# A list of experts ordered by token quarters in 15 classes; pieces that serve one quarter as plain fp32 products of 64 columns, two side by side

## The chip, the cores and the metric

The kernel runs on one core of a Trainium2 chip. The metric is the time of one execution on the device in microseconds. An execution is profiled apart from the timed ones, and its trace gives for every engine when each instruction ran.

## What is computed

Two transformer blocks over 256 tokens of width 2048, all in float32. The last part of the second block is the one that the change touches: a layer of 16384 single-neuron experts, of which each token uses 128 (8 heads with 16 each).

```python
def peer_ffn(hn, w_query, sub_keys, expert_down, expert_up):
    ...
    top_s, top_i = lax.top_k(scores, PEER_TOPK)
    cand_s = (top_s[:, :, 0, :, None] + top_s[:, :, 1, None, :]).reshape(...)
    cand_i = (top_i[:, :, 0, :, None] * PEER_N_KEYS + top_i[:, :, 1, None, :]).reshape(...)
    best_s, best_pos = lax.top_k(cand_s, PEER_TOPK)
    expert_idx = jnp.take_along_axis(cand_i, best_pos, axis=-1)
    gates = jax.nn.softmax(best_s, axis=-1)
    ...
        u = expert_down[idx]
        act = jax.nn.gelu(jnp.einsum('thkd,td->thk', u, xb), approximate=False)
        vv = expert_up[idx]
        return jnp.einsum('thk,thkd->td', (gb * act).astype(vv.dtype), vv)
```

## The kernel before

The kernel computes the expert layer densely where it can. A matrix G holds the gate of each token for each expert (zero where the token doesn't use it); all down projections are computed (jobs on `w_pd`, tile A4), and U is the product of activation and gate, turned so that a row is one expert with 256 tokens. The output is U times the up weights `w_pu`, a sum over experts in pieces of 128 rows of 2048 floats (1 MB).

Experts that no token uses are left out. `table_gen` notes which experts each half of the tokens uses (tiles `used0`, `used1`). `rank_gen` gives every expert a place in a list: first those that only the first half (tokens 0 to 127) uses, then those of both, then those of the second alone, then the unused. `u_gen` scatters each row of U to its place in a buffer in DRAM by an indirect DMA of GpSimd (L1716, 124 of them), each row with the expert's number behind its 256 values. The last four pieces of experts (`dense`) are not scattered.

The list is then worked off in 105 pieces (`UP_C`). Pieces 0 to 27 serve the first half alone, 28 to 76 both, 77 to 104 the second alone, whatever the data; if the classes don't fit these bounds, a flag `bad` is set and a branch behind the list, `all_experts`, computes everything anew. For each piece:

- SyncE loads 128 rows of the list (`urow`, L1799, 130 KB); seven buffers, up to two pieces ahead of the next step.
- GpSimd gathers the up weights of these experts with the numbers in `urow` (L1809, 1 MB, tile `ring`, six buffers).
- ScalarE and VectorE split both into a high and a low part in fp32r (`A5hi`, `A5lo`, L1830 and L1831; `wh`, `wl`, L1835 and L1836), three steps ahead of TensorE; a step is half a piece, 1024 of its columns.
- TensorE makes three fp32r products (low by high, high by high, high by low) of 128 by 512 for each of the four column blocks and each half of the tokens that the piece serves: 12 products for a piece and a half (`up_run`, L1863 to L1865). They add up in eight PSUM banks, four (`mm`) for the first half of the tokens and four (`aux`) for the second.

When the last product of a bank is done, `finish` adds the residual and stores the result. TensorE begins the stage with the four dense pieces (tile `ulast`), beside which the first pieces of the list are loaded. The instruction `memset` on L1820 is the fence behind which rows may be read from the list.

An engine runs its instructions in the order in which the code issues them. Side work (`rank_gen`, `u_gen`) is written as generators; `pump` advances each by one `yield` after every step of TensorE's main work.

Of the kernel before, what the change touches and what calls it, by code (L numbers as in the profile page):

```python
# [19 lines left out]
P = 128  # L20
# [19 lines left out]

UP_A, UP_B, UP_C = 77, 28, 105
TRASH = UP_C * P
# [139 lines left out]
class _Up:  # L182


    kc, before = 4, None

    def __init__(self, c, tiles, dense=False):
        self.c, self.tiles, self.dense = c, tiles, dense


@with_exitstack
def tile_kernel(ctx: ExitStack, tc: tile.TileContext, T, out):
# [83 lines left out]
    def run_jobs(jobs):  # L276
        units = []
        for j in jobs:
            for u in range(j.kc // 2):
                units.append((j, u))  # L280
        order = [j for j in jobs if isinstance(j, _Job) or j.dense]
        held = []
# [23 lines left out]
        def split(s):  # L306
            j, u = units[s]
            if isinstance(j, _Up) and not j.dense:
                sp[s] = up_split(j, u)
# [20 lines left out]
        for s, (j, u) in enumerate(units):  # L330
# [6 lines left out]
            if u == 0 and j.before is not None:  # L337
                j.before()
            wh, wl = sp.pop(s)
            if isinstance(j, _Up):  # L340
                if room == len(units):
# [1021 lines left out]
    def open_peer():  # L1363
# [11 lines left out]
        for n in ("i1T", "i2T", "gaT"):  # L1375
            pk[n] = pre.tile([P, S], F32, name=n)
        pk["F"] = [mp.tile([P, P], F32, name=f"used{t}") for t in range(2)]
        pk["st1"] = ExitStack()
# [132 lines left out]
    def table_gen():  # L1511

        with ExitStack() as es:
# [38 lines left out]
            def used(n):  # L1552
                per = S // TB // 2
                if n % per == 0:
                    dve.tensor_copy(acc, st["s", n])
                else:
                    dve.tensor_tensor(acc, acc, st["s", n], op=ALU.max)

            N = S // TB
            for n in range(N + 4):  # L1560
# [15 lines left out]
                if n < N:  # L1576
                    first(n)
                if n - 3 in (N // 2 - 1, N - 1):
                    for w in (4, 2):
                        dve.tensor_tensor(acc[:, :w], acc[:, :w], acc[:, w:2 * w], op=ALU.max)  # L1580
                    t = 0 if n - 3 < N // 2 else 1
                    F = pk["F"][t]
# [6 lines left out]
    def rank_gen():  # L1589


        spare = [pk["post"].tile([P, 8, P], F32, tag="gt", name=nm("spare"), bufs=6) for _ in range(2)]
        sl = lambda k: slice(k * P, (k + 1) * P)
        lt, b, far, over, s = (spare[0][:, k] for k in range(5))
        end = spare[0][:, 5, :1]
        e = spare[0][:, 6, :3]
        rs, ct = (spare[1][:, 3 * k:3 * k + 3].rearrange("p k c -> p (k c)") for k in range(2))
        d = rs
        F0, F1 = pk["F"]
        dve.tensor_tensor(b, F0, F1, op=ALU.mult)  # L1600
        dve.tensor_tensor(F0, F0, b, op=ALU.subtract)
        dve.tensor_tensor(F1, F1, b, op=ALU.subtract)
        cls = (F0, b, F1)
        rp, tp = aux(), aux()
        for k in range(3):
            pe.matmul(rp[:, sl(k)], cls[k], ones, start=True, stop=True)
        for k in range(3):
            pe.transpose(tp[:, sl(k)], cls[k], ident)
        yield
        act.copy(rs, rp[:, :3 * P])  # L1610
        act.copy(ct, tp[:, :3 * P])
        dve.tensor_tensor(lt, triu, ident, op=ALU.subtract)

        dve.tensor_copy(far, pk["ids"])
        dve.tensor_scalar(far, far, float(TRASH), None, op0=ALU.add)
        gp, np_ = aux(), aux()
        for k in range(3):
            pe.matmul(gp[:, sl(k)], cls[k], lt, start=True, stop=False)
            for q in range(k):
                pe.matmul(gp[:, sl(k)], ones, rs[:, sl(q)], start=False, stop=False)  # L1620
            pe.matmul(gp[:, sl(k)], lt, rs[:, sl(k)], start=False, stop=True)

        for k in range(3):
            for q in range(k + 1):
                pe.matmul(np_[:, sl(k)], ones, rs[:, sl(q)], start=q == 0, stop=q == k)
        yield

        dve.tensor_scalar(d, gp[:, :3 * P], float(-TRASH), None, op0=ALU.add)
        dve.tensor_tensor(d, d, ct, op=ALU.mult)
        dve.tensor_tensor(s, d[:, sl(0)], d[:, sl(1)], op=ALU.add)  # L1630
        dve.tensor_tensor(s, s, d[:, sl(2)], op=ALU.add)
        yield
        dve.tensor_scalar(over, s, 0.0, None, op0=ALU.is_ge)
        dve.tensor_scalar(s, s, 0.0, float(TRASH), op0=ALU.min, op1=ALU.add)
        dve.tensor_tensor(far, far, s, op=ALU.subtract)
# [4 lines left out]
        yield  # L1640
        dve.tensor_scalar(e[:, 0:1], np_[:, 0:1], float(UP_B * P), None, op0=ALU.is_lt)
        dve.tensor_scalar(e[:, 1:2], np_[:, P:P + 1], float(UP_A * P), None, op0=ALU.is_gt)
        dve.tensor_scalar(e[:, 2:3], np_[:, 2 * P:2 * P + 1], float(UP_C * P), None, op0=ALU.is_gt)
        dve.tensor_reduce(end, e, axis=AX.X, op=ALU.max)
        dve.tensor_copy(pk["bad"], end)

# [144 lines left out]

    up = {"loaded": 0, "rows": 0}
# [11 lines left out]
    def up_load(upto):  # L1804
        while up["loaded"] <= min(upto, len(ups) - 1):
            j = ups[up["loaded"]]
            rows_load(up["loaded"] + 2)
            j.raw = ring()
# [4 lines left out]
    def up_split(j, u):  # L1813
        if "fence" not in pk:
# [9 lines left out]
        e = ups.index(j)  # L1824
        if u == 0:
            up_load(e + 3)
            a, b = j.tiles[0] * P, (j.tiles[-1] + 1) * P

            j.hi, j.lo = (x[:, 0] for x in xt_tiles("A5", e % 4))
            act.copy(j.hi[:, a:b], j.u[:, a:b])  # L1830
            dve.tensor_tensor(j.lo[:, a:b], j.u[:, a:b], j.hi[:, a:b].bitcast(F32), op=ALU.subtract)  # L1831
        src = j.raw[:, u * 1024:(u + 1) * 1024]
        wh = wpool.tile([P, 1024], F32R, tag="wh", name=nm("wh"), bufs=4)
# [3 lines left out]
        return wh, wl  # L1837

    def up_run(j, u, wh, wl, tiles):
        if j.dense:  # L1840
            k = 0
            while "ulast" not in pk:
                pump()
                k += 1
                assert k < 1000
            hi, lo = (x[:, j.c - JL] for x in pk["ulast"])
        else:
            hi, lo = j.hi, j.lo
        if j is ups[-3] and u == 0:
            pk["over"] = nc.values_load(pk["bad"][0:1, 0:1], min_val=0, max_val=1)  # L1850
        for t in tiles:
            mine = [x for x in dense + ups if t in x.tiles]
            first, last = j is mine[0], j is mine[-1]
            if first and u == 0:
# [59 lines left out]


    alone = [_Up(c, (0,)) for c in range(UP_B)], [_Up(c, (1,)) for c in range(UP_A, UP_C)]
    both = [_Up(c, (0, 1)) for c in range(UP_B, UP_A)]
    dense = [_Up(JL + k, (0, 1), True) for k in range(4)]
    mid = alone[0][4:] + alone[1][:-4]
    ups = alone[0][:4]  # L1920
    while both or mid:
        ups += both[:1] + mid[:1]
        both, mid = both[1:], mid[1:]
    ups += alone[1][-4:]
    jobs += dense + ups
    run_jobs(jobs)
# [30 lines left out]
```

## Time and profile before

| | us |
|---|---|
| median of 3 runs | 3033.9 |
| lowest and highest | 3032.38, 3033.99 |
| the profiled execution's own time | 3032.62 |
| its span, first to last instruction | 3030.7 |
| TensorE busy in the span | 3006.2 (99%) |
| VectorE, ScalarE, GpSimd busy | 2013.5, 1652.9, 432.0 |

The span is read against the profiled execution's own time, which is 1.9 us longer. Times in the trace count from the span's start. A busy engine is one with an instruction in work; matmuls overlap, so the step from one start to the next, not the length of one, is what TensorE pays.

### The profile page before, as it was taken

The page shows a single profiled execution, that of the slowest core. Times are in us where ns is not written, and L with a number is a line of the kernel's source. Part 1 is how long each engine was busy: PE and PEld are TensorE (multiplying, and loading weights), DVE is VectorE, ACT ScalarE, POOL GpSimd, SP SyncE. Part 2 cuts the span into 40 slices and gives each one's busy share as a digit, 9 for nine tenths or more (in the row PEclk, how much of TensorE's full clock was granted, in tenths as well). Part 3 has the DMA queues.
Part 4 walks back from the last instruction along what each step waited for, and adds up shares of the span by engine and source line. Part 5 has one row for each costly group of instructions (what it writes and reads, how often), then busy time and mean ns, then how long its engine had stood idle before and what let it go on. Part 6 is the DMA issues. An engine that isn't in the chain of part 4 may idle for free. (4 is left out here: it accounts for less than half of the span.)

```text
span 3030.7 us, 39602 instructions
## 1 busy us (share of the span) xinstructions
PE 3006.2 (99%) x14715; PEld 2576.3 (85%) x14715; DVE 2013.5 (66%) x2890; ACT 1652.9 (55%) x2426; POOL 432.0 (14%) x496
## 2 busy tenths in 40 slices
PE   9999999999999999999999999999999999999998
PEld 7899988888888888898998888888888888888887
DVE  6876655566555557567656689877875555666666
ACT  7455545544444445565555544447774554555555
POOL 2310000000000000103111000000002664333332
PEclk9999999999999999999999999999999999999999
DMA  7344555555555555554455687666777997888886
GB/s 293 118 141 163 183 177 183 191 194 181 194 182 194 189 186 169 193 182 148 142 177 180 233 275 256 220 209 210 221 212 247 341 343 270 317 292 292 287 292 213
DMA packets 161868, 658.27 MB, mean 217 GB/s; under 512 B 15488, under 2 KB 63232, under 8 KB 103040
## 3 DMA queue, kind: packets, MB, share of 16 engines
q1 hardware_dynamic: 95808, 491.37, 47.9%
q0 software_dynamic: 21072, 126.62, 11.3%
q10 hardware_dynamic: 44784, 37.64, 3.7%
q8 instruction: 118, 1.93, 0.2%
q14 instruction: 86, 0.70, 0.1%
HBM read 600.97 MB, written 54.60 MB: 216 GB/s over the span
## 5 line engine op out<-in xcount | busy, mean ns | idle before, releaser
L325 DVE TENSOR_TENSOR wl<-raw,wh 128x1024 fp32r<-128x1024 f32 (+2 forms) x902 | 1061.8, 1180 | 822.8 <-ACT wh L324 778.3
L324 ACT CAST wh<-raw 128x1024 fp32r<-128x1024 f32 (+2 forms) x902 | 901.6, 1003 | 937.1 <-PE mm L374 866.9
L373 PE MATMUL mm<-wh,A4lo 128*128 128x512 f32 x1152 | 459.7, 399 | 0.0
L375 PE MATMUL mm<-wl,A4hi 128*128 128x512 f32 x1152 | 449.6, 390 | 0.0
L374 PE MATMUL mm<-wh,A4hi 128*128 128x512 f32 x1152 | 448.8, 390 | 0.0
L1836 DVE TENSOR_TENSOR wl<-ring,wh 128x1024 fp32r<-128x1024 f32 x210 | 256.9, 1226 | 142.1 <-ACT wh L1835 134.8
L1835 ACT CAST wh<-ring 128x1024 fp32r<-128x1024 f32 x210 | 219.9, 1050 | 179.4 <-PE aux L1864 154.7
L373 PE MATMUL mm<-wh,A2lo 128*128 128x512 f32 x704 | 274.4, 390 | 0.0
L375 PE MATMUL mm<-wl,A2hi 128*128 128x512 f32 x704 | 274.0, 389 | 0.0
L374 PE MATMUL mm<-wh,A2hi 128*128 128x512 f32 x704 | 273.9, 389 | 0.0
L375 PEld LDWEIGHTS mm<-wl,A4hi 128*128 128x128 f32 x1152 | 216.2, 188 | 46.5
L374 PEld LDWEIGHTS mm<-wh,A4hi 128*128 128x128 f32 x1152 | 216.8, 188 | 41.7
L373 PEld LDWEIGHTS mm<-wh,A4lo 128*128 128x128 f32 x1152 | 216.7, 188 | 41.1
L1716 POOL DMA_INDIRECT U<-ut,tgt x124 | 137.6, 1109 | 750.4 <-DVE ut L1706 633.1
L373 PE MATMUL mm<-wh,A1lo 128*128 128x384 f32 (+2 forms) x512 | 185.1, 361 | 1.8 <-ACT wh L324 1.8
L1809 POOL DMA_INDIRECT ring<-in_w_pu_dram,urow x105 | 143.5, 1367 | 265.7 <-DVE A5lo L1831 203.0
L375 PE MATMUL mm<-wl,A1hi 128*128 128x384 f32 (+2 forms) x512 | 179.9, 351 | 0.5 <-DVE wl L325 0.5
L374 PE MATMUL mm<-wh,A1hi 128*128 128x384 f32 (+2 forms) x512 | 179.3, 350 | 0.0
L373 PE MATMUL mm<-wh,A3lo 128*128 128x384 f32 (+2 forms) x448 | 158.9, 355 | 0.0
L375 PE MATMUL mm<-wl,A3hi 128*128 128x384 f32 (+2 forms) x448 | 154.1, 344 | 2.0 <-DVE wl L325 1.9
L375 PEld LDWEIGHTS mm<-wl,A2hi 128*128 128x128 f32 x704 | 132.2, 188 | 27.5
L374 PEld LDWEIGHTS mm<-wh,A2hi 128*128 128x128 f32 x704 | 132.2, 188 | 27.3
(484 smaller groups left out, 5396.4 us busy)
## 6 DMA issues: line engine op xcount, KB each, us to landing
raw<-in_w_pd_dram SPq DMA_DIRECT2D x128, 1024.0 KB, 5.6
raw<-in_w_gate_dram SPq DMA_DIRECT2D x44, 1024.0 KB, 4.8
raw<-in_w_up_dram SPq DMA_DIRECT2D x44, 1024.0 KB, 4.8
raw<-in_w_down_dram SPq DMA_DIRECT2D x44, 1024.0 KB, 4.8
raw<-in_w_in_c_dram SPq DMA_DIRECT2D x44, 768.0 KB, 4.4
raw<-in_w_out_dram SPq DMA_DIRECT2D x32, 1024.0 KB, 4.9
raw<-in_w_in_s_dram SPq DMA_DIRECT2D x32, 768.0 KB, 4.2
raw<-in_w_ple_gate_dram SPq DMA_DIRECT2D x16, 1024.0 KB, 4.8
```

Source lines behind the costliest of these rows:

```text
L324: act.copy(wh[:, c], src[:, c])
L325: dve.tensor_tensor(wl[:, c], src[:, c], wh[:, c].bitcast(F32), op=ALU.subtract)
L373: pe.matmul(ps[t][:, :n], ll, a, start=st, stop=False)
L374: pe.matmul(ps[t][:, :n], lh, a, start=False, stop=False)
L375: pe.matmul(ps[t][:, :n], lh, b, start=False, stop=en)
L1716: i = pool.indirect_dma_start(pk["U"][:, :], bass.IndirectOffsetOnAxis(ap=pk["tgt"][:, j:j + 1], axis=0), s["u"][:, q, :], None).ins
L1809: pool.indirect_dma_start(j.raw, None, T["w_pu"], bass.IndirectOffsetOnAxis(ap=j.u[:, S:S + 1].bitcast(U32), axis=0))
L1835: act.copy(wh, src)
L1836: dve.tensor_tensor(wl, src, wh.bitcast(F32), op=ALU.subtract)
```

## The change

The tokens are cut into four quarters of 64 and each expert has a class by the set of quarters that use it (a number from 1 to 15). The list is ordered by the 15 classes in the sequence `CLASSES`, chosen so that each quarter is served by few windows of pieces (`WINDOWS`). A piece then serves, for each half of the tokens, both quarters (`full`, as before: three fp32r products of 128 by 512), one quarter (`single`), or none. A single quarter is computed by one plain float32 product per column block, whose stationary operand is the 64 columns of `urow` for that quarter and whose moving operand is the raw gathered tile: no split on ScalarE and VectorE. Quarters 0 and 2 write the lower 64 partitions of a bank, quarters 1 and 3 the upper 64, and a step of class `_Pair` takes one of each kind, mostly of two pieces, and issues their products in turn.

The numbers give 105 pieces: 42 with one quarter, 27 with two single quarters, 18 with a full half and one quarter, 14 with one full half, 4 with two full halves. They make 72 steps on full halves (40 piece and half combinations) and 57 pairs; the pairs stand in 17 runs between full steps, so that the kind of step changes 34 times. Before, there are 154 piece and half combinations and no other kind.

```diff
-UP_A, UP_B, UP_C = 77, 28, 105
+CLASSES = (2, 10, 8, 9, 13, 5, 1, 3, 11, 15, 7, 6, 14, 12, 4)
+UP_C = 105
+WINDOWS = (((28, 76),), ((0, 18), (57, 87)), ((35, 47), (68, UP_C)), ((11, 40), (64, 72), (82, 94)))
+RING = 9
...
+    cost = lambda p: 2.72 * len(p.full) + 1.72 * len(p.single)
+    mean = sum(map(cost, rest)) / len(rest)
...
+        def score(p):
+            b = bal + sum(1 if q % 2 == 0 else -1 for q in p.single)
+            return (100.0 if abs(b) > 2 else 0.3 * abs(b)) + abs(spent + cost(p) - mean * (len(order) + 1))
+        p = min(rest, key=score)
...
+        if p.full:
+            steps += [_Full(p, u) for u in range(2)]
+        for q in p.single:
+            side[q % 2].append((p, q))
+        pairs(2)
...
     def rows_load(upto):
-        while up["rows"] <= min(upto, len(ups) - 1):
-            j = ups[up["rows"]]
-            j.u = pk["post"].tile([P, UW], F32, tag="urow", name=nm("urow"), bufs=7)
-            i = nc.sync.dma_start(j.u, pk["U"][j.c * P:(j.c + 1) * P, :]).ins
+        while up["rows"] <= min(upto, len(pieces) - 1) and free(up["rows"]):
+            n = up["rows"]
+            if n % RING < 7:
+                u = pk["post"].tile([P, UW], F32, tag="urow", name=nm("urow"), bufs=7)
+            else:
+                u = pk["post"].tile([P, 4, UW], F32, tag="ut", name=nm("urow"), bufs=2)[:, 0]
+            pieces[n].u = u
+            i = nc.sync.dma_start(u, pk["U"][pieces[n].c * P:(pieces[n].c + 1) * P, :]).ins
...
+    free = lambda n: n < RING or not pieces[n - RING].left
...
+            j.raw = ring() if n % RING < R else wpool.tile([P, 2048], F32, tag="raw", name=nm("raw"), bufs=3)
...
+    def step_run(j, wh, wl):
...
+        if isinstance(j, _Full):
+            p = j.pieces[0]
+            product(p.hi, p.lo, j.u, wh, wl, p.full, False, p is pieces[-1])
+        else:
+            for i in range(4):
+                for k, (p, q) in enumerate(j.sides):
+                    n = i ^ k
+                    pe.matmul(acc[q // 2][n][q % 2 * 64:(q % 2 + 1) * 64], p.u[:, q * 64:(q + 1) * 64],
+                              p.raw[:, n * 512:(n + 1) * 512], start=False, stop=False)
+        for p in j.pieces:
+            p.left -= 1
+        up_load()
```

`rank_gen` now works on four tiles `used` and 15 masks: the counts of each class by 15 products with one column, the places within a class by 15 products of 128 by 128, and on VectorE 15 comparisons and 15 selections of 128 by 128 where there were three of each kind. It passes seven yields before the places are known, where it passed three. `table_gen` closes a group of tokens four times instead of twice. The branch `all_experts` stays, with a test for each of the 15 window edges.

On TensorE, where the first pair of the list stands, these rows belong to a pair: `ring` and `raw` are gathered up weights, `urow` rows of the list, and `mm` and `aux` the banks of the first and second half of the tokens. Of the program with the change:

```order
L2008 MATMUL mm_21692<-wh_21968,A5lo_21955 128x512
L2009 MATMUL mm_21692<-wh_21968,A5hi_21954 128x512
L2010 MATMUL mm_21692<-wl_21969,A5hi_21954 128x512
L1982 MATMUL mm_21689<-ring_21810,urow_21800 64x512
L1982 MATMUL aux_21734<-ring_21810,urow_21800 64x512
L1982 MATMUL mm_21690<-ring_21810,urow_21800 64x512
L1982 MATMUL aux_21733<-ring_21810,urow_21800 64x512
L1982 MATMUL mm_21691<-ring_21810,urow_21800 64x512
L1982 MATMUL aux_21736<-ring_21810,urow_21800 64x512
L1982 MATMUL mm_21692<-ring_21810,urow_21800 64x512
L1982 MATMUL aux_21735<-ring_21810,urow_21800 64x512
```

Before, the list's products are all of this form, here those of the first step of a piece:

```order
L1863 MATMUL mm_21595<-wh_21726,A5lo_21723 128x512
L1864 MATMUL mm_21595<-wh_21726,A5hi_21722 128x512
L1865 MATMUL mm_21595<-wl_21727,A5hi_21722 128x512
L1863 MATMUL mm_21596<-wh_21726,A5lo_21723 128x512
L1864 MATMUL mm_21596<-wh_21726,A5hi_21722 128x512
L1865 MATMUL mm_21596<-wl_21727,A5hi_21722 128x512
```

Three products of 128 columns per bank have become one of 64 columns per bank, and two such products that stand next to each other write different halves of the partitions in different banks.

On GpSimd, at the start of the list, the gathers with the change, each behind the row load of the same piece on SyncE:

```order
L1938 DMA ring_21818<-in_w_pu_dram,urow_21808 128x2048
L1938 DMA ring_21822<-in_w_pu_dram,urow_21812 128x2048
L1938 DMA raw_21826<-in_w_pu_dram,urow_21816 128x2048
L1938 DMA raw_21828<-in_w_pu_dram,urow_21820 128x2048
L1938 DMA raw_21830<-in_w_pu_dram,urow_21824 128x2048
L1938 DMA ring_21914<-in_w_pu_dram,urow_21912 128x2048
```

The same place before:

```order
L1809 DMA ring_21720<-in_w_pu_dram,urow_21710 128x2048
L1809 DMA ring_21760<-in_w_pu_dram,urow_21714 128x2048
L1809 DMA ring_21794<-in_w_pu_dram,urow_21718 128x2048
L1809 DMA ring_21822<-in_w_pu_dram,urow_21758 128x2048
```

Nine pieces instead of six have a buffer, three of them in tiles that held the dense weights. A row load now has the same ring of nine as its gather, where it ran ahead of it before.

Ahead of the list nothing moves on TensorE but the products of `rank_gen`: the 31 groups of transposes of `u_gen` stand between the same products of the down projections as before, and the dense pieces between the same transposes.

## Rows read from the trace of the kernel before

**Rows 1.** The page: span, busy time and share of each engine.

```profile
span 3030.7 us, 39602 instructions
PE 3006.2 (99%) x14715; PEld 2576.3 (85%) x14715; DVE 2013.5 (66%) x2890; ACT 1652.9 (55%) x2426; POOL 432.0 (14%) x496
```

**Rows 2.** Windows of 50 us over the list: engines' busy time, clock, DMA share, GB/s.

```profile
2600.00:2650.00 50.00, 49.25 (x216) 40.11 (x215) 37.14 (x42) 32.35 (x43) 15.72 (x15) 1.00 0.98 391
2650.00:2700.00 50.00, 50.00 (x223) 41.39 (x222) 32.36 (x37) 29.13 (x37) 17.71 (x13) 1.00 0.82 291
...
2950.00:3000.00 50.00, 50.00 (x222) 41.42 (x221) 33.17 (x38) 28.64 (x38) 18.16 (x13) 1.00 0.81 284
```

**Rows 3.** Timeline of TensorE: start, length; first dense product, list's first and last.

```profile
2579.05 0.40 PE L1863 MATMUL mm<-wh,ulast 128*128 128x512 f32 x1
...
2602.70 0.50 PE L1863 MATMUL mm<-wh,A5lo 128*128 128x512 f32 x1 [0.23 <-ACT wh L1835]
2603.04 0.40 PE L1864 MATMUL mm<-wh,A5hi 128*128 128x512 f32 x1
2603.96 0.50 PE L1865 MATMUL mm<-wl,A5hi 128*128 128x512 f32 x1 [0.53 <-DVE wl L1836]
...
3022.30 0.39 PE L1865 MATMUL aux<-wl,A5hi 128*128 128x512 f32 x1
```

**Rows 4.** Groups of TensorE's instructions in the list (busy us, mean ns, idle before).

```profile
L1863 PE MATMUL mm<-wh,A5lo 128*128 128x512 f32 x308 | 119.9, 389 | 0.2 <-ACT wh L1835 0.2
L1865 PE MATMUL aux<-wl,A5hi 128*128 128x512 f32 x308 | 119.8, 389 | 0.0
L1863 PEld LDWEIGHTS aux<-wh,A5lo 128*128 128x128 f32 x308 | 57.8, 188 | 12.0
```

**Rows 5.** Timeline of TensorE around a plain float32 product with 512 moving columns (L1234).

```profile
1423.49 0.33 PE L375 MATMUL mm<-wl,A3hi 128*128 128x384 f32 x1
1423.67 1.02 PE L1234 MATMUL aux<-t,btok 128*128 128x512 f32 x2
1423.50 0.36 PEld L1234 LDWEIGHTS aux<-t,btok 128*128 128x128 f32 x2
1424.12 0.74 PE L373 MATMUL mm<-wh,A3lo 128*128 128x384 f32 x1
1424.70 0.34 PE L374 MATMUL mm<-wh,A3hi 128*128 128x384 f32 x1
1424.87 0.34 PE L375 MATMUL mm<-wl,A3hi 128*128 128x384 f32 x1
```

**Rows 6.** Windows of 10 us at the start of the list, columns as in Rows 2.

```profile
2610.00:2620.00 10.00, 10.00 (x46) 8.28 (x45) 9.31 (x12) 7.37 (x11) 2.87 (x3) 1.00 1.01 408
2620.00:2630.00 10.00, 10.00 (x46) 8.29 (x45) 6.53 (x8) 6.43 (x9) 4.11 (x4) 1.00 1.02 412
2640.00:2650.00 10.00, 10.00 (x46) 8.28 (x45) 6.93 (x8) 5.18 (x9) 3.86 (x4) 1.00 0.83 299
```

**Rows 7.** Timeline of GpSimd: the fence, the first gather, and gathers in between.

```profile
2590.46 0.09 POOL L1820 MEMSET pjunk<- 1x8 f32 x1 [1.83 <-issue]
2592.90 1.34 POOL L1809 DMA_INDIRECT ring<-in_w_pu_dram,urow  x1 [2.35 <-DMA urow<-U]
2594.55 0.96 POOL L1809 DMA_INDIRECT ring<-in_w_pu_dram,urow  x1 [0.30 <-DMA urow<-U]
2595.81 0.94 POOL L1809 DMA_INDIRECT ring<-in_w_pu_dram,urow  x1 [0.30 <-DMA urow<-U]
...
2614.49 0.94 POOL L1809 DMA_INDIRECT ring<-in_w_pu_dram,urow  x1 [3.50 <-DMA urow<-U]
...
2634.57 0.94 POOL L1809 DMA_INDIRECT ring<-in_w_pu_dram,urow  x1 [1.92 <-DMA urow<-U]
```

**Rows 8.** DMA issues of the page, and time to landing of the gathers.

```profile
urow<-U SPq DMA_DIRECT2D x105, 130.0 KB, 4.9
DMA to landing us min/median/max: 5.9/7.7/15.5
```

**Rows 9.** Waits from 2592 us on: who waited for whom, us in total, times, longest.

```profile
POOL ring L1809 <- DVE A5lo L1831: 203.0, 48, 4.8
ACT wh L1835 <- PE aux L1864: 154.7, 123, 1.7
```

**Rows 10.** Groups of VectorE and ScalarE in the list.

```profile
L1836 DVE TENSOR_TENSOR wl<-ring,wh 128x1024 fp32r<-128x1024 f32 x210 | 256.9, 1226 | 142.1 <-ACT wh L1835 134.8
L1835 ACT CAST wh<-ring 128x1024 fp32r<-128x1024 f32 x210 | 219.9, 1050 | 179.4 <-PE aux L1864 154.7 <-DMA ring<-in_w_pu_dram,urow 11.7 <-PE mm L1864 7.4
```

**Rows 11.** Timelines of TensorE and VectorE around the ranking.

```profile
2300.92 0.39 PE L1621 MATMUL aux<-spare,spare 128*128 128x128 f32 x2
2301.15 0.39 PE L1618 MATMUL aux<-spare,used 128*128 128x128 f32 x2
2295.44 0.28 DVE L1600 TENSOR_TENSOR spare<-used,used 128x128 f32<-128x128 f32 x1
```

More of the change, by code (lines that the diff above doesn't have):

```diff
@@ L182, with __init__ @@
 class _Up:
-    kc, before = 4, None
-    def __init__(self, c, tiles, dense=False):
-        self.c, self.tiles, self.dense = c, tiles, dense
+    kc, before, dense, tiles = 4, None, True, (0, 1)
+    def __init__(self, c):
+        self.c = c
+class _Piece:
+    def __init__(self, c, mask):
+        self.c, self.left = c, 0
+        two = [mask >> 2 * t & 3 for t in range(2)]
+        self.full = tuple(t for t in range(2) if two[t] == 3)
+        self.single = [2 * t + two[t] - 1 for t in range(2) if two[t] in (1, 2)]
@@ new lines, with __init__, _limits @@
+class _Full:
+    kc, before, dense = 2, None, False
+    def __init__(self, piece, u):
+        self.pieces, self.u = (piece,), u
+class _Pair:
+    kc, before, dense = 2, None, False
+    def __init__(self, sides):
+        self.sides = sides
+        self.pieces = [p for p, q in sides]
+def _limits():
+    lim = []
+    for q in range(4):
+        w = list(WINDOWS[q])
+        for k, c in enumerate(CLASSES):
+            on, was = c >> q & 1, k > 0 and CLASSES[k - 1] >> q & 1
+            if on and not was and k:
+                lim.append((k - 1, w[0][0] * P, True))
+            if on and not (k + 1 < len(CLASSES) and CLASSES[k + 1] >> q & 1):
+                lim.append((k, w.pop(0)[1] * P, False))
+        assert not w
+    return lim
@@ new lines, in _pieces_order, with pairs @@
+def _pieces_order():
+    mask = [sum(1 << q for q in range(4) if any(a <= c < b for a, b in WINDOWS[q])) for c in range(UP_C)]
+    rest = [_Piece(c, m) for c, m in enumerate(mask)]
+    end = [p for p in rest if len(p.full) == 2][-1]
+    rest.remove(end)
+    cost = lambda p: 2.72 * len(p.full) + 1.72 * len(p.single)
+    mean = sum(map(cost, rest)) / len(rest)
+    order, steps, side, spent = [], [], ([], []), 0.0
+    bal = 0
+    def pairs(least):
+        while min(map(len, side)) >= least:
+            for _ in range(min(map(len, side))):
+                steps.append(_Pair([side[0].pop(0), side[1].pop(0)]))
+    while rest:
+        def score(p):
+            b = bal + sum(1 if q % 2 == 0 else -1 for q in p.single)
+            return (100.0 if abs(b) > 2 else 0.3 * abs(b)) + abs(spent + cost(p) - mean * (len(order) + 1))
+        p = min(rest, key=score)
+        rest.remove(p)
+        order.append(p)
+        spent += cost(p)
+        bal += sum(1 if q % 2 == 0 else -1 for q in p.single)
+        if p.full:
[3 more added lines that the diff above has]
+        pairs(2)
+    pairs(1)
+    steps += [_Pair([x]) for k in range(2) for x in side[k]]
+    order.append(end)
+    steps += [_Full(end, u) for u in range(2)]
+    for x in steps:
+        for p in x.pieces:
+            p.left += 1
+    return order, steps
@@ L280, in run_jobs @@
                 units.append((j, u))
-        order = [j for j in jobs if isinstance(j, _Job) or j.dense]
+        order = [j for j in jobs if isinstance(j, (_Job, _Up))]
         held = []
@@ L307, in split @@
             j, u = units[s]
[L308 to L309 removed]
+            if isinstance(j, (_Full, _Pair)):
+                sp[s] = up_split(j)
                 return
@@ L1376, in open_peer @@
             pk[n] = pre.tile([P, S], F32, name=n)
-        pk["F"] = [mp.tile([P, P], F32, name=f"used{t}") for t in range(2)]
+        pk["F"] = [mp.tile([P, P], F32, name=f"used{t}") for t in range(4)]
         pk["st1"] = ExitStack()
@@ L1602, in rank_gen @@
[L1602 to L1608, printed above, removed]
-        yield
-        act.copy(rs, rp[:, :3 * P])
-        act.copy(ct, tp[:, :3 * P])
-        dve.tensor_tensor(lt, triu, ident, op=ALU.subtract)
+        rows_ = [pk["post"].tile([P, UW], F32, tag="urow", name=nm("rank"), bufs=7) for _ in range(4)]
@@ new lines, in rank_gen @@
+        dve.tensor_copy(ends, bp[:, P:P + K])
+        place(0, p0)
+        p1, p2 = within(1), within(2)
+        yield
+        place(1, p1)
+        place(2, p2)
+        p3 = within(3)
+        mine(range(4))
+        yield
+        place(3, p3)
+        mine(range(4, 12))
+        yield
+        mine(range(12, K))
+        dve.tensor_tensor(spare[0][:, :7], spare[0][:, :7], spare[1][:, :7], op=ALU.add)
+        for n in (4, 2, 1):
+            dve.tensor_tensor(spare[0][:, :n], spare[0][:, :n], spare[0][:, n:2 * n], op=ALU.add)
@@ L1640, in rank_gen @@
         yield
[L1641 to L1645, printed above, removed]
+        lim = _limits()
+        for n, (k, v, behind) in enumerate(lim):
+            dve.tensor_scalar(e[:, n:n + 1], ends[:, k:k + 1], float(v), None, op0=ALU.is_lt if behind else ALU.is_gt)
+        dve.tensor_reduce(over[:, :1], e[:, :len(lim)], axis=AX.X, op=ALU.max)
+        dve.tensor_copy(pk["bad"], over[:, :1])
     scatters = []
@@ L1802, in rows_load, with up_load @@
             up["rows"] += 1
[L1804 to L1808, printed above, removed]
+    def up_load():
+        while up["loaded"] < len(pieces) and free(up["loaded"]):
+            n = up["loaded"]
+            rows_load(n + 2)
+            j = pieces[n]
+            j.raw = ring() if n % RING < R else wpool.tile([P, 2048], F32, tag="raw", name=nm("raw"), bufs=3)
             pool.indirect_dma_start(j.raw, None, T["w_pu"],
@@ L1837, in up_split, with product @@
         return wh, wl
-    def up_run(j, u, wh, wl, tiles):
[L1840 to L1850, printed above, removed]
+    def step_run(j, wh, wl):
+        if j is steps[-3]:
+            pk["over"] = nc.values_load(pk["bad"][0:1, 0:1], min_val=0, max_val=1)
+        if isinstance(j, _Full):
+            p = j.pieces[0]
+            product(p.hi, p.lo, j.u, wh, wl, p.full, False, p is pieces[-1])
[7 more added lines that the diff above has]
+            p.left -= 1
+        up_load()
+    def up_run(j, u, wh, wl, tiles):
+        k = 0
+        while "ulast" not in pk:
+            pump()
+            k += 1
+            assert k < 1000
+        hi, lo = (x[:, j.c - JL] for x in pk["ulast"])
+        product(hi, lo, u, wh, wl, tiles, j is dense[0], False)
+    def product(hi, lo, u, wh, wl, tiles, first, last):
         for t in tiles:
-            mine = [x for x in dense + ups if t in x.tiles]
-            first, last = j is mine[0], j is mine[-1]
             if first and u == 0:
@@ L1913, in tile_kernel @@
         jobs += [_Job(T["w_pd"][g, k], 4, 512, ("A4", k), k == 0, k == 3, down_evac(g)) for k in range(4)]
[L1916 to L1925, printed above, removed]
+    dense = [_Up(JL + k) for k in range(4)]
+    pieces, steps = _pieces_order()
+    jobs += dense + steps
     run_jobs(jobs)
```

101 lines of the change are left out of this document (63 added, 38 removed).

## Prediction

> **What bounds the kernel now.** First the head of the page: TensorE is busy for 99% of the span, VectorE for 66%, ScalarE for 55% [rows 1]. So it is TensorE's own work that has to shrink. Then the stage that the change rewrites, in windows of 50 us: TensorE has no idle time after the first of them, its clock is granted in full, and the transfers take 0.81 to 0.98 of the DMA engines' time [rows 2]. The timeline gives the stage its edges: the first product of the list starts at 2602.70, the last at 3022.30, with 0.76 us of idle time in the first step [rows 3]. These 419.8 us (to the last product's end, less the 0.16 us by which a product outlasts the step to the next) hold 154 combinations of piece and token half, 12 products each: 0.227 us a product, 2.72 us a combination. The length of one, 389 ns, is not its price, since products overlap [rows 4]. The waits confirm the reading: ScalarE waits for TensorE to give buffers back (154.7 us), GpSimd for VectorE (203.0 us), and TensorE for almost nothing [rows 4, 9].
>
> **What goes.** 154 combinations become 40: 114 times 2.72 us, 310 us less on TensorE. VectorE and ScalarE lose two thirds of their large splits, 210 to 72 [rows 10]; this is worth nothing by itself, since both had idle time.
>
> **What comes on TensorE.** 57 pairs of 8 plain float32 products with 512 moving columns. The trace has this product with 128 stationary columns (L1234): two records, 1.02 us from start to end, and the stream behind it tells the price. L374 starts at 1424.70; at the steady step of 0.17 its forerunner should have started at 1424.53, so the product took 1424.53 - 1423.67 = 0.86 us [rows 5], 3.8 times a split product. What no row shows is two products in the two halves of the array at once. From below, a pair costs 4 times 0.86 = 3.42 us (each half pays its own four, wholly beside the other's); from above 8 times 0.86 = 6.84 us (one after another). I take 3.42. The nearest row is L1234 itself: each of its two records occupies the array for 0.43 us, the second record's weights are loaded while the first runs (both loads end at 1423.86 [rows 5]), and products of this kernel show that loads of weights (188 ns) hide beside running products [rows 4]. With two records to a product and strict order, the second record of one side can run beside the first of the other, so a run of pairs loses one record, 0.43 us, at its start: 17 runs, 7 us (an estimate). The sum is 40 x 2.72 + 57 x 3.42 = 108.8 + 194.9 = 303.7 us, 115 less than 418.9; with the run starts 108 less.
>
> The Trainium skill ("TensorE: Matmul & The Clock Gate", Part 3: Packing small matmuls) has three column tiles of 32 reach 2.38 times the rate of one, that is 0.79 of each tile's share. By it a pair here would gain 1.59 and cost 4.3 us, and the sum would be 51 us worse; no run here shows it yet.
>
> **The change of kind.** 34 times the array goes from 128 columns to 64 or back. If the pipeline has to run empty first, each costs at most what a product outlasts its step: 0.39 - 0.23 = 0.16 us [rows 3], together 5.6 us; at least nothing. I take 3. The Trainium skill ("TensorEngine Tiling (Array Packing)", Key Properties) says that a change of tiling mode drains the engine, which would put it at the upper end.
>
> **What comes of the transfers.** They don't shrink: 105 pieces of 1 MB and 130 KB as before, now in some 310 us instead of 420. In the 10 us windows from 2610 to 2630, when the ring first fills, the DMA share is 1.01 and 408 to 412 GB/s are moved, against 299 later [rows 6]. In the same stretch the gathers start every (2634.57 - 2614.49) / 7 = 2.87 us [rows 7] (eight gathers, the six between are left out), and 1.18 MB in 2.87 us is that rate: this is what the engines can do. 105 x 2.87 = 301 us, from the first gather at 2592.90 [rows 7] to about 2894, the last landing some 6 us later, 2900; the last piece's 2.3 us of split [rows 10] and 5.4 us of products put a floor at about 2908 under the stage's end. TensorE's own 2602.7 + 303.7 + 7 + 3 = 2916 is above it, but only by 8 us: the two now run nearly level, and any unevenness is a wait.
>
> The ring decides how many. Before, a piece's buffers were free as soon as it was split. Now a piece with a single quarter holds `ring` and `urow` until TensorE is through with its pair, and its row load can't run ahead of its buffer any more: row 4.9 us, 1.25 us from one gather to the next on GpSimd, gather 7.7 us [rows 7, 8] make 13.9 us from a freed slot to new data. Nine slots at 2.9 us a piece turn over in 26 us, so some 12 us, four pieces' worth, remain for lying ready and being used. I went through the 105 pieces in their order by these prices (a slot reloads when its ninth forerunner's last step ends; landings no closer than 2.87): TensorE waits 11 us in all with 4.0 for a row and 6 for a gather, 17 with 4.9 and 6, 27 with 4.9 and 7.7. The smallest gather took 5.9 and the median 7.7 under a 0.82 load [rows 2, 8]; queueing is in the 2.87 already, so I take 17.
>
> **The ranking.** VectorE runs some 36 small operations more at about 0.28 us [rows 11], 10 us over eight steps, in a stretch where splits stand three steps (8 us) ahead of TensorE; that cover hides them, and without it at most 10 us would be lost. TensorE pays 15 products of one column and 15 of 128 for 18 of 128 before. One of 128 costs 2301.15 - 2300.92 = 0.23 us [rows 11]; one of a column can't undercut its two loads of weights, about 0.2. So 7.3 us against 4.4: 3 us more. The places come four steps (11 us) later; the scatters then have some 270 us until the fence [rows 7, 11], and all of `u_gen` on TensorE stands where it stood, so that the stage begins when it did.
>
> **Sum.** -115 + 7 + 3 + 17 + 3 = -85 us, on 3032.62 of the profiled execution 2947.6, and with the median 1.3 us higher 2948.9. The forecast is **2948 us.** If this case holds, its own range is 2920 (no waits, no cost at the changes) to 2967 (27 us of waits, 6 at the changes).
>
> **Rivals.**
> *The loads of weights don't hide.* If the 64-column loads of one side can't run beside the other side's products, each of the 8 slots of a pair gets longer by half to all of a 128-column load, 0.09 to 0.19 us [rows 4]: 4.2 to 4.9 us a pair, 44 to 84 us more, of which 5 to 8 come back as the waits for transfers shrink. 2985 to 3023 us, about 3000. For it: a plain product's loads are two where a split product's is one. Against: the second load of L1234 cost nothing visible [rows 5]. The Trainium skill ("TensorE: Matmul & The Clock Gate", Part 3, The mechanism) has loads run beside products only where their row groups differ, which those of the two halves don't; by that rule this rival would be the likeliest. The trace speaks against the rule for whole-array products, whose loads of 188 ns lie within steps of 227 ns [rows 3, 4], so its chance stays below that of the full overlap.
>
> *The halves don't run side by side at all.* A pair costs 6.84, the stage 108.8 + 389.9 = 498.7 us, 80 more than 418.9, and with the ranking and the changes of kind 86: about 3118 us, slower. The point at which it turns is a pair of 3.42 + (85 + 8) / 57 = 5.1 us, an overlap of a third. For it: no product of this trace runs beside another for more than its 0.16 us of tail. Against: nothing in the trace either; different banks and different partitions are written, so the results needn't meet.
>
> *The slots starve.* If row and gather reach their longest under full load (15.5 us for a gather [rows 8]), a slot turns over in 4.9 + 1.25 + 15.5 + 12.2 = 33.9 us, 3.8 us a piece, 395 for the list, and it ends at 2593 + 395 + 8 = 2996 instead of 3022.7. Halfway between this and my case: about 2980.
>
> *The list doesn't fit its windows.* Then `all_experts` runs behind it: 2 x 128 pieces x 12 products x 0.227 = 697 us more, 3640. No row of the trace shows the counts of the classes. By the reference's arithmetic they depend on how small a gate still counts as used: the edges hold by 10 experts or more if gates under some e^-93 to e^-98 vanish, and are missed by 13 to 28 if all count or if the smallest normal float is the limit.
>
> **How the numbers follow.** Side by side in full 0.57, loads exposed 0.18, no overlap 0.15, starved slots 0.06, no fit 0.04. Faster by over 0.2% (6 us, about what a measurement of this kernel can tell from no change): all of the first and the fourth case and most of the second, 0.79; within 0.2% the second's upper edge, 0.01; slower the third, the fifth and the rest, 0.20. The range has to leave out no more than 0.2: the two slow cases (0.19) stay outside, the exposed loads stay in. 2920 to 3028.
>
> **What would show it.** Right: records of the pair's products that overlap two by two, with starts 0.43 us apart for two records; a stage of about 330 us; a DMA share near 1.0 in it; waits of TensorE for `ring`, `raw` and `urow` of 10 to 27 us in all. Wrong: starts of the 64-column products 0.43 apart one by one (no overlap) or steps of 0.5 to 0.6 for two (loads exposed); TensorE idle by 50 us or more with the DMA share well below 1 (starved slots); rows of `all_experts`. If the dense pieces start later than 2579.05 [rows 3], the ranking was not hidden.

## The result, and the profile after

The median after is 2962.85 us (2958.62 to 2965.21), before 3033.41 us: a ratio of 0.9766 with a 95% interval of 0.9749 to 0.9783, 70.6 us less. The forecast was 2948 us, its range 2920 to 3028. The profiled execution took 2965.21 us with a span of 2963.4, which stands against [rows 1]. One of the six executions of *rows ahead* below took 4171.48 us at a granted clock of 0.65 and isn't in the range given there (without it the median is 2934.92). This is the head of the page after:

```profile
span 2963.4 us, 38111 instructions
PE 2916.4 (98%) x14287; PEld 2391.6 (81%) x14287; DVE 1835.3 (62%) x2741; ACT 1491.5 (50%) x2233; POOL 400.4 (14%) x497
```

TensorE is busy for 89.8 us less, and the span is only 67.3 us shorter: the rest is idle time that was not there. The windows of 50 us say where (columns as in [rows 2]):

```profile
2650.00:2700.00 50.00, 50.00 (x231) 20.50 (x231) 5.72 (x7) 4.18 (x5) 15.72 (x17) 1.00 1.00 391
2700.00:2750.00 50.00, 48.54 (x224) 17.09 (x222) 2.65 (x3) 2.29 (x3) 15.93 (x17) 1.00 1.02 404
2750.00:2800.00 50.00, 45.31 (x196) 19.88 (x194) 13.10 (x16) 11.26 (x16) 15.70 (x16) 0.97 0.97 373
2800.00:2850.00 50.00, 43.84 (x186) 20.64 (x184) 13.00 (x15) 11.27 (x15) 12.16 (x13) 0.93 0.81 307
2850.00:2900.00 50.00, 45.64 (x193) 22.51 (x190) 14.74 (x17) 13.26 (x18) 13.36 (x13) 0.97 0.91 342
2900.00:2950.00 50.00, 46.85 (x193) 26.08 (x192) 13.80 (x16) 11.19 (x14) 11.86 (x11) 0.93 0.67 263
```

For 100 us (2650 to 2750) the new products run without a gap or nearly so, with the transfers at their limit. From 2750 on TensorE waits and the DMA share falls below 1 in the same windows. So the rate of the transfers can't be what is waited for there; something holds back their start. The granted clock falls with TensorE's waits, to 0.93.

**The pairs.** TensorE's timeline where a run of pairs begins, behind split products:

```profile
2652.82 0.39 PE L2010 MATMUL aux<-wl,A5hi 128*128 128x512 f32 x1
2653.14 0.64 PE L1982 MATMUL mm<-ring,urow 128*64 128x512 f32 x1
2653.15 0.64 PE L1982 MATMUL aux<-ring,urow 128*64 128x512 f32 x1
2653.62 0.59 PE L1982 MATMUL mm<-ring,urow 128*64 128x512 f32 x1
2653.63 0.59 PE L1982 MATMUL aux<-ring,urow 128*64 128x512 f32 x1
2654.05 0.59 PE L1982 MATMUL mm<-ring,urow 128*64 128x512 f32 x1
2654.05 0.59 PE L1982 MATMUL aux<-ring,urow 128*64 128x512 f32 x1
```

Two records, one for each half of the array, start within 0.01 us of each other, and the next two 0.43 us later. In the whole list none of the 912 records of pairs runs alone, so 57 pairs take 456 slots of 0.4285 us, 3.43 us a pair. The first slot starts 0.32 us after the last split product where a split product would start 0.23 after it, and the second slot 0.48 us after the first where 0.43 is the rule: 0.14 us for the change of kind. The way back, at the end of the same run:

```profile
2659.63 0.59 PE L1982 MATMUL mm<-raw,urow 128*64 128x512 f32 x1
2659.63 0.59 PE L1982 MATMUL aux<-raw,urow 128*64 128x512 f32 x1
2660.16 0.50 PE L2008 MATMUL aux<-wh,A5lo 128*128 128x512 f32 x1
2660.49 0.40 PE L2009 MATMUL aux<-wh,A5hi 128*128 128x512 f32 x1
```

The first split product starts 0.10 us later than a next slot would, the second 0.11 later than the steady step, and the steps behind it lose 0.03 more until they are steady: 0.24 us. The weights that TensorE loads for the pairs are hidden; here is their group beside that of a split product's, the counterparts to the last line of [rows 4]:

```profile
L1982 PEld LDWEIGHTS aux<-ring,urow 128*64 128x64 f32 x312 | 35.4, 137 | 39.8 <-issue 39.8
...
L2008 PEld LDWEIGHTS aux<-wh,A5lo 128*128 128x128 f32 x84 | 16.8, 200 | 19.0 <-ACT wh L1968 11.0 <-issue 4.1 <-ACT A5hi L1963 0.8
```

**The waits.** This is the chain of waits in the second half of the list, its long pieces around two of TensorE's waits (start, length, what):

```profile
2812.44 7.85 DMA urow<-U
...
2822.32 8.41 DMA ring<-in_w_pu_dram,urow
2830.82 1.05 ACT wh L1968
2831.92 0.80 PE mm L2008
...
2863.91 10.38 DMA urow<-U
2874.33 0.72 issue
2875.05 0.93 POOL raw L1938
2876.03 0.52 issue
2876.75 8.99 DMA raw<-in_w_pu_dram,urow
2885.84 1.05 ACT wh L1968
2886.92 1.27 DVE wl L1969
2888.23 0.79 PE aux L2010
```

Read from top to bottom: a row load of 7.85 us, then a gather of 8.41, then ScalarE's split, then TensorE. GpSimd issues the gathers one after the other, so the row load in the chain is each time that of the piece before: the gather of that piece waits for it, and the next gather stands behind. By the landings in the trace a piece itself takes, from the start of its own row load to its landed weights, 17.9 us the first time (2812.86 to 2830.72) and 18.9 the second (2866.86 to 2885.74). From the tenth piece on, where slots are used again, the median is 17.8; the prediction had 13.9. The issues of transfers in this stretch (count, KB, median us to landing) say that this is no exception, against 4.9 and 7.7 in [rows 8]:

```profile
urow<-U SPq DMA_DIRECT2D x105, 130.0 KB, 7.3
...
ring<-in_w_pu_dram,urow POOLq DMA_INDIRECT x72, 9.0
```

And the waits turn round: in [rows 9] ScalarE waited for TensorE, now for the gathers, and GpSimd for the rows.

```profile
ACT wh L1968 <- DMA ring<-in_w_pu_dram,urow: 129.7, 25, 10.0
POOL ring L1938 <- DMA urow<-U: 102.7, 32, 10.9
```

What a wait costs TensorE is more than its idle time, as its timeline behind the wait of 2886 shows:

```profile
2886.94 0.50 PE L2008 MATMUL aux<-wh,A5lo 128*128 128x512 f32 x1 [2.09 <-ACT wh L1968]
2887.28 0.46 PE L2009 MATMUL aux<-wh,A5hi 128*128 128x512 f32 x1
2888.23 0.79 PE L2010 MATMUL aux<-wl,A5hi 128*128 128x512 f32 x1 [0.49 <-DVE wl L1969]
2888.82 0.63 PE L2008 MATMUL aux<-wh,A5lo 128*128 128x512 f32 x1
2889.25 0.63 PE L2009 MATMUL aux<-wh,A5hi 128*128 128x512 f32 x1
2889.68 0.63 PE L2010 MATMUL aux<-wl,A5hi 128*128 128x512 f32 x1
```

The products start 0.43 us apart instead of 0.227: from 2888.2 to 2890.9 the granted clock is 0.50, the lower of its two levels (1.2 instead of 2.4 GHz); from 2891 on it is 1.00 again.

**The account.** From the list's first product to its last it is 2954.50 - 2609.39 = 345.1 us, against 419.6 [rows 3]. In it lie 480 x 0.2266 + 456 x 0.4285 = 304.2 us of products, 27.5 us in 21 places where a step is over 0.3 us longer than the steady one, 5.9 us for changes of kind (17 into pairs, 14 back; the other three ways back lie within the 21 places), and 5.7 us in 29 steps of about 0.43 between split products in the lower clock. The last 2 us are mostly the first steps behind waits. Eight of the 21 places are steps of 0.59 to 0.67 us in the lower clock right behind a wait, so that some 2 of the 27.5 us belong to the clock as well. The list begins 6.7 us later than before, and what follows its last product is 0.4 us longer: -74.5 + 6.7 + 0.4 = -67.4 us, the difference of the spans but for rounding.

### The profile page after: what moved, and what is told of

Read it like the earlier page. It is cut to its first block, busy times and chain, and to the rows that moved or that the text cites. A ratio compares the mean times of both kernels' runs of the same rounds, so it can differ in the third digit from the quotient of the medians.

```text
span 2963.4 us, 38111 instructions
## 1 busy us (share of the span) xinstructions
PE 2916.4 (98%) x14287; PEld 2391.6 (81%) x14287; DVE 1835.3 (62%) x2741; ACT 1491.5 (50%) x2233; POOL 400.4 (14%) x497
## 5 line engine op out<-in xcount | busy, mean ns | idle before, releaser
L1837 POOL DMA_INDIRECT U<-ut,tgt x124 | 144.9, 1169 | 148.7 <-issue 52.3
L466 PEld LDWEIGHTS mm<-wl,A2hi 128*128 128x128 f32 x704 | 132.1, 188 | 27.5
L464 PEld LDWEIGHTS mm<-wh,A2lo 128*128 128x128 f32 x704 | 132.2, 188 | 27.3
L465 PE MATMUL mm<-wh,A3hi 128*128 128x384 f32 (+2 forms) x448 | 153.7, 343 | 0.0
L1969 DVE TENSOR_TENSOR wl<-ring,wh 128x1024 fp32r<-128x1024 f32 x56 | 66.3, 1223 | 128.8 <-ACT wh L1968 128.5
```

The source lines that it names most:

```text
L464: pe.matmul(ps[t][:, :n], ll, a, start=st, stop=False)
L465: pe.matmul(ps[t][:, :n], lh, a, start=False, stop=False)
L466: pe.matmul(ps[t][:, :n], lh, b, start=False, stop=en)
L1837: i = pool.indirect_dma_start(pk["U"][:, :], bass.IndirectOffsetOnAxis(ap=pk["tgt"][:, j:j + 1], axis=0), s["u"][:, q, :], None).ins
L1969: dve.tensor_tensor(wl, src, wh.bitcast(F32), op=ALU.subtract)
```

## The experiments

In what follows "waits" is the sum of all steps of TensorE in the list that are over 0.3 us longer than the steady one, less the steady one, as in the account.

**One side after the other.** All four products of one side of a pair are issued before those of the other.

```diff
-            for i in range(4):
-                for k, (p, q) in enumerate(j.sides):
+            for k, (p, q) in enumerate(j.sides):
+                for i in range(4):
```

> The four products of one side of a pair are issued before the four of the other, nothing else changes. Theory A (the engine starts products in the order of issue, and two run beside each other only when neighbours in that order write different halves): only the last product of one side meets the first of the next, a pair rises from 3.43 us to about 6.0 to 6.4, and the time by 57 x 2.6 to 3.0 less some 35 us of waits and slow clock that vanish: 3075 to 3100 us. Rival B (each half of the array has a queue of its own that runs ahead): records still start two by two 0.43 us apart and the time stays at 2963 within 5 us.

Measured: 2978.28 us (one execution), between the two theories and far nearer to B. The timeline at the start of a run (a number behind x counts records that one line stands for):

```profile
2653.33 2.36 PE L1982 MATMUL mm<-ring,urow 128*64 128x512 f32 x5
2655.10 0.64 PE L1982 MATMUL aux<-ring,urow 128*64 128x512 f32 x1
2655.52 0.59 PE L1982 MATMUL mm<-ring,urow 128*64 128x512 f32 x1
2655.58 0.59 PE L1982 MATMUL aux<-ring,urow 128*64 128x512 f32 x1
```

The first side runs four slots alone; then the other joins it, though eight records of the first stand ahead of its own in the program, and they go on two by two. At the end of the run the second side is left alone for as long. So 8 of a run's records are alone, 136 in 17 runs, and 68 slots more are needed: 29 us. Some 95 steps between slots within the runs are 0.49 us instead of 0.43 besides, 5 us; 16 us come back as the waits shrink (11.8 left) and 4 of the lower clock. A product of one half of the array need not wait until all products ahead of it in the program have started: some four slots of work of the other half may stand before it.

**The same bank.** Both sides of a pair write the same column block, so the two halves of one bank where both serve the same half of the tokens.

```diff
-                    n = i ^ k
+                    n = i
```

> The two sides of a pair go through the column blocks in the same order (n = i instead of n = i ^ k), so that two sides of the same token half write two halves of the partitions of the same bank at once. Theory A (partitions, not banks, decide): steps of 0.43 us for two records, time 2963 within 5 us. Rival B (one bank takes one product at a time): those pairs whose sides belong to the same token half step by 0.86 us for two records, up to 57 x 3.4 us more, above 3000 us.

Measured: 2963.68 us (one execution). In 27 of the 57 pairs both sides serve the same half of the tokens, so that each of their 216 slots writes one bank: in these too the two records start 0.00 to 0.01 us apart and the slots step by 0.43. Which bank is written makes no difference; the exchange of banks in the change buys nothing.

**Rows ahead.** The rows get a ring of fifteen of their own (in parts of tiles that lie there unused), and are asked for six pieces ahead of the gather instead of two. The nine slots for weights stay.

```diff
-        while up["rows"] <= min(upto, len(pieces) - 1) and free(up["rows"]):
+        while up["rows"] <= min(upto, len(pieces) - 1) and (up["rows"] < 15 or not pieces[up["rows"] - 15].left):
...
-            rows_load(n + 2)
+            rows_load(n + 6)
```

> The row loads get a ring of fifteen (all four parts of the two wide tiles are used) and run up to six pieces ahead of the gathers; the gathers keep their nine buffers. Theory A (the list waits for slots whose turnover is row load, then gather, one after the other, 7 to 10 us and 7 to 11 us): the row load leaves the turnover, TensorE's waits in the list fall from 27.5 us to under 10, the slow clock behind them from some 10 us to under 4, the time falls by 20 to 32 us to 2931 to 2943. Rival B (the DMA engines are full, so it doesn't matter when rows are fetched): 2963 within 6 us.

Measured: 2935.0 us (2934.7 to 2935.7), a ratio of 0.9677 (0.9664 to 0.9689) to before, 27.9 us below the change as it stands. Theory A holds. The windows:

```profile
2700.00:2750.00 50.00, 50.00 (x232) 17.67 (x230) 2.85 (x4) 2.49 (x4) 15.18 (x16) 1.00 1.02 412
2750.00:2800.00 50.00, 49.68 (x222) 23.34 (x218) 15.38 (x18) 13.15 (x18) 17.94 (x17) 1.00 1.02 410
2800.00:2850.00 50.00, 50.00 (x223) 22.25 (x222) 17.90 (x21) 15.35 (x21) 19.23 (x17) 1.00 1.01 405
2850.00:2900.00 50.00, 50.00 (x224) 26.29 (x223) 15.47 (x19) 13.49 (x18) 18.35 (x17) 1.00 0.98 381
```

TensorE is full and so, until 2850, are the DMA engines: the waits are 4.0 us, 3.5 of them at the first pieces, and the clock stays at 1.00. The list takes 316.2 us, 28.9 less; 23.5 of that are waits, and the rest is the lower clock behind them (one step of 0.43 is left of 29; the 10 us of the expectation were the whole remainder of the account). What holds GpSimd back is now mostly TensorE, which gives slots back, and no longer the rows, for which it waits 25.8 us instead of 151.7:

```profile
POOL ring L1942 <- PE aux L1986: 70.3, 16, 7.8
```

**Eight slots.** The ring of the change with eight slots instead of nine for rows and weights alike.

```diff
-RING = 9
+RING = 8
```

> Eight pieces in the ring instead of nine. Theory A (turnover of slots): nine slots give about 30 us of turnover at the measured pace, eight would allow 11% less work per turnover, waits rise by 10 to 30 us, time 2973 to 2995. Rival B (DMA rate alone): 2963 within 6 us.

Measured: 2986.42 us, ratio 0.9844 (0.983 to 0.9858), waits of 45.7 us and a list of 367.8 us. In time it is 23.6 us more than with nine slots. As long as a slot's time holds a row load and a gather, each slot counts.

**Rows ahead with eight slots.** The last two edits together.

> The row ring of fifteen with eight buffers for the weights instead of nine. Theory A (once rows run ahead, a freed slot only waits for its gather of 8 to 9 us, so slots are no longer what limits): 2934 to 2945 us, waits of TensorE in the list below 12 us. Theory B (the number of slots still decides, as it did between the rings of eight and nine without rows ahead, 23.6 us apart): 2950 to 2965 us.

Measured: 2939.78 us (2937.46 to 2941.99), waits of 5.9 us. Theory A: the ninth slot is worth 23.6 us with the row load in the chain, and 4.8 without it.

**Rows three ahead.** The ring of fifteen, asked for three pieces ahead.

```diff
-            rows_load(n + 2)
+            rows_load(n + 3)
```

> The row ring of fifteen, but rows are asked for only three pieces ahead of the gather instead of six. Theory A (what counts is that a row's load of 7 to 10 us begins before its weights' slot is free; three pieces at 2.9 us cover it): 2935 to 2942 us, waits of TensorE in the list below 10 us. Theory B (rows have to lie far ahead, or it is the deeper queue of loads that helps): 2945 to 2960 us.

Measured: 2935.45 us (one execution), waits of 4.2 us. One piece more of lead and a buffer that doesn't depend on the weights' slot suffice together; six pieces bring nothing more. Neither was tried without the other.

**No pairs.** Pieces that serve one quarter of a half are treated as serving both, so that everything runs as split products.

```diff
-        self.full = tuple(t for t in range(2) if two[t] == 3)
-        self.single = [2 * t + two[t] - 1 for t in range(2) if two[t] in (1, 2)]
+        self.full = tuple(t for t in range(2) if two[t])
+        self.single = []
```

> The list in its 15 classes with nine slots, but a piece that serves one quarter of a half is treated as serving both: split products of 128 columns, no pairs, 154 combinations as before the change. Theory A (all of the gain is in the pairs; order, ranking and ring bring none and the transfers hide beside 419 us of products): the list takes 418 to 421 us and begins 6 to 7 us late, 3037 to 3043 us, 4 to 9 slower than before the change. Theory B (the new ring or the order has a part in the gain): below 3030 us.

Measured: 3041.41 us (3039.94 to 3043.38), ratio 1.0027 (1.0017 to 1.0038): slower than before by 0.27%. TensorE's first and last product of the list:

```profile
2610.72 0.39 PE L2008 MATMUL mm<-wh,A5lo 128*128 128x512 f32 x1
...
3030.11 0.39 PE L2010 MATMUL aux<-wl,A5hi 128*128 128x512 f32 x1
```

419.4 us as before, and a start 8.0 us later than in [rows 3] (up to 7 were expected). All of the gain lies in the pairs; order, ring and ranking by themselves cost 8 us.

**Wide counts.** With rows ahead, the counts of the ranking take 32 columns instead of one. The reason: behind the 30 one-column records of the ranking, eight split products start 0.43 us apart in the changed kernel.

```diff
-            pe.matmul(rp[:, k:k + 1], C[k], ones[:, :1], start=True, stop=True)
-        pe.transpose(rp[:, P:2 * P], w, ident)
+            pe.matmul(rp[:, 32 * k:32 * k + 32], C[k], ones[:, :32], start=True, stop=True)
+        wp = aux()
+        pe.transpose(wp[:, :P], w, ident)
...
```

> The row ring of fifteen, and the 15 count products of the ranking with 32 columns instead of one; their transposes in a tile of their own. Theory A (the one-column products are why the clock is granted at half for the eight split products behind them): the split products behind the counts start 0.23 us apart instead of 0.43, the 30 records take about as long as before (3.3 us), the list starts 1 to 2 us earlier than with the one-column products, 2933 to 2934 us. Theory B (it is the kind of product, plain float32, or the loads of weights, and not the width): the half clock stays, 2935 us or, if 32 columns make a record longer, up to 2938.

Measured: 2935.7 us (2934.38 to 2938.02). Theory B holds; the timeline at and behind the counts is as with one column.

```profile
2300.28 3.43 PE L1701 MATMUL aux<-cst,spare 128*128 128x32 f32 x30
2303.54 0.31 PE L1703 MATMUL aux<-cst,rank 128*128 128x128 f32 x1
...
2304.73 0.63 PE L464 MATMUL mm<-wh,A4lo 128*128 128x512 f32 x1
2305.16 0.63 PE L465 MATMUL mm<-wh,A4hi 128*128 128x512 f32 x1
```

30 records take 3.3 us at either width, 0.11 us each. My theory of the single column fell; what the lower clock behind these products comes from stays open.

## Why the prediction was right, and where it was off

**What goes and what comes on TensorE: right.** 304.2 us of products against 303.7 in the prediction. The price of a pair, 3.42 us at the lower bound, measures 3.43; the pairs alone make the gain (without them nothing but the 8 us of cost is left).

**Run starts: 7 us forecast, 0 measured.** "With two records to a product and strict order, the second record of one side can run beside the first of the other, so a run of pairs loses one record": the order isn't strict between the halves, and that an engine runs its instructions in the order of issue, as I wrote of the kernel before, doesn't hold between them. The experiment with one side after the other shows the same from the other end, since the second side overtakes.

**Change of kind: mis-sized,** 3 us forecast, 5.6 at most. 5.9 were measured, and 6.6 with rows ahead, where no wait lies on any of the 34. A change costs 0.14 us into pairs and 0.24 back, 0.19 in the mean. The bound, "each costs at most what a product outlasts its step" (0.16), fits the step across the change, which is 0.09 to 0.10 us longer, but leaves out the steps behind it, which lose as much again. The page that I named for it in the Trainium skill ("TensorEngine Tiling (Array Packing)", Key Properties) has a change drain the engine; the trace agrees in that each change costs, at the upper end and a little above.

**Waits for transfers: mis-sized.** "TensorE waits [...] 17 with 4.9 and 6, 27 with 4.9 and 7.7. [...] queueing is in the 2.87 already, so I take 17." 27.5 were measured, at the upper end, and 5.7 us for the lower clock behind them, which the sum didn't have at all. The step that failed is the price of a slot's turnover, 13.9 us, and with 6 for a gather even less: in the changed kernel's trace it is 17.8 in the median, 17.9 and 18.9 in the two waits shown, since the row load takes 7.3 us in the median and up to 10.4 in the chain, and the gather 9.0. That the 27 us of the dearer prices come so near is chance: the trace doesn't have those prices either, and 3 of the 27.5 us lie at the first pieces, before any slot is used again. Row load and gather were priced from a stage with a DMA share of 0.82 and used for one with 1.00. That the row load in the slot's chain is the cause was shown by taking it out (27.9 us); that with a load of 4.9 us it would have been harmless is only argued. The two bounds of the prediction, TensorE at 2916 and the transfers at 2908, are what rows ahead comes near to: its last product starts at 2924.01.

**The ranking: 3 forecast, 5.5 measured.** Matched product by product to the trace before, the down projections are 1.3 us late ahead of the ranking already, as they are from their first product at 1690 us on, and 6.8 behind it. TensorE's counts and the half clock behind them (about 1.6 us) are in this, and about 1.1 us in which TensorE waits for VectorE's `gt` at 2334 to 2335, where the cover that should hide the 36 small operations seems a little short. That leaves 2.8 us for the products that the forecast had at 3 (its own prices, 0.23 and 0.2, give 6.5 against 4.1, so 2.3). From the counts to the first dense product it is 285.9 us in all nine traces with the new ranking, so that this part is steady; what differs from one to another, up to 3.5 us, lies ahead of it.

**The rivals.** No overlap and a list that doesn't fit are out: pairs run side by side, and no product of `all_experts` stands behind the list. *The loads of weights don't hide* is out as well: two loads of 137 ns lie in each slot of 0.43 us. For the Trainium skill ("TensorE: Matmul & The Clock Gate", Part 3), neither point weighed ahead holds here: two halves reach twice the rate of one for these products, where the estimate from its three column tiles of 32 was 1.59 times, and loads hide though the row groups are the same. *The slots starve* had the right place, the slot's turnover; the measured 17.8 us lie halfway between my 13.9 and its 4.9 + 1.25 + 15.5 = 21.7, so it was the neighbour of my case rather than another mechanism.

**How near the sum came.** In the sum, 7 us of run starts that never came made up for part of what was priced too low: 10.5 us of waits, 5.7 of clock, 3 of changes and 2.5 of ranking, with some 3 us more in steps behind waits and in the late start. So the profiled execution lies 17.6 us above the 2947.6 of the sum: 25 us of misses, less 7 that went the other way by luck. The case's own range doesn't follow from the terms named beside it either: no waits and no cost at the changes make 2929 us, 27 and 6 us make 2962, where it says 2920 and 2967.

## What to carry to other kernels

Where a change makes TensorE as fast as the transfers beside it, price each transfer at the load that the stage will then have, and add up the whole chain from a freed buffer to its next use: here a small load of 130 KB in front of the large one cost 28 us of a gain of 98, and a buffer of its own for it brought that back. Put into a wait on TensorE also what the lower clock takes behind it.

## What was not expected of the hardware

- Plain float32 products of 64 stationary columns in the two halves of the array run side by side in full, 0.43 us for two records with 512 moving columns, also into the same bank (216 slots; 2963.68 against 2962.85 us).
- A change between these products and split products of the whole array costs 0.14 us one way and 0.24 the other, half of it in the steps behind the change (2653.14 to 2653.62 and 2660.16 to 2660.49).
- The halves are not held to the program's order between them: a record issued behind eight of the other half's joined after four slots (2653.33 and 2655.10).
- After some waits of about 2 to 6 us, and after the 30 short plain float32 records of the counts, the clock was granted at its lower level (0.50 from 2888.2 to 2890.9 and from 2303.8 to 2307.2 us), and split products started 0.43 us apart instead of 0.227 for a few products (eight, behind the counts).
- With the DMA engines at a share of 1.01 to 1.02 the transfers moved 405 to 412 GB/s for 150 us beside a TensorE that was busy for 149.7 of them (rows ahead, 2700 to 2850).
